# A hybrid attention layer: the second weight group is summed and split within the first projection step, two tiles of x are scaled next, and the rotation tables are loaded later

## The chip, the cores and the metric

The kernel runs on one core of a Trainium2 chip. TensorE (PE) multiplies matrices, VectorE (DVE), ScalarE (ACT) and GpSimd (POOL) do the elementwise work, SyncE (SP) issues transfers; sixteen DMA engines move the data. The metric is the device time of one execution in microseconds (us), the median of several.

## The reference

One layer over 1024 positions of width 1024, in float32:

```python
h = _rmsnorm(x, norm_gain[l])
proj = h @ w_in[l]
q_a, k_a, v_a, g_a, q_b, k_b, v_b, g_b = jnp.split(proj, split_at, axis=-1)
q_a = _rmsnorm(q_a.reshape(b, s, A_HEADS, HEAD_DIM), q_norm_a[l])
k_a = _rmsnorm(k_a.reshape(b, s, A_KV_HEADS, HEAD_DIM), k_norm_a[l])
q_a = q_a * cos + _rotate_half_axial(q_a) * sin
k_a = k_a * cos + _rotate_half_axial(k_a) * sin
o_a = _gqa_blocked(q_a, k_a, v_a) * jax.nn.silu(g_a)
o_b = _neighbourhood_attn(q_b, k_b, v_b, na_rpb[l]) * jax.nn.silu(g_b)
x = x + jnp.concatenate([o_a, o_b], axis=-1) @ w_out[l]
return _rmsnorm(x, final_norm_gain)
```

Group A is full attention with 8 query heads and 2 key heads, with normalised and rotated queries and keys. Group B is attention over a neighbourhood of a 16 x 64 grid. All that the change touches lies before the first scores of group A.

## The kernel before, in words

To keep float32 accuracy with float16 matmuls, every operand is split in two float16 parts: a high part (a scaled copy, rounded) and a low part (what the rounding left). A product is three matmuls: high by high, high by low, low by high.

The 1024 rows of x are eight tiles, numbered 0 to 7, of 128 rows. A tile passes through `load_x` (a transfer of 512 KB, SP's queue), `x_sq` (sum of squares, L289), `x_rs` (L296 on VectorE, then a power and a factor on POOL, L297 and L298), `x_y` (scaling on VectorE, L301; the high part on ScalarE, L302) and `x_lo` (the low part, L306). Each part is transposed by a transfer on SP's queue (`x_t`, L310) into `hT0` (high) or `hT1` (low). Four buffers hold tiles of x, so tile 4's load waits until tile 0 is done with.

The projection's 3328 columns are 13 groups of 256 (`raw0`, `raw1`, ... as loaded, `whl` as split). Preparing a group takes `prep_a` (squares, summed along a row: L344, L347, L364), `prep_b` (a matmul that adds the sums over the partitions, L373; then L375 on VectorE and a power on POOL, L376), `prep_c` (high parts on ScalarE, L382), `prep_d` (low parts on VectorE, L389) and `prep_e` (a few small factors, L421 to L428). From group 3 on the squares are L357 and the halves are split in quarters (L399, L404). Two buffers hold loaded groups and two hold split ones; group 2's split takes the place of group 0's. `load_w` (L207, POOL's queue, 1 MB) fetches groups from 2 on; for groups 2 and 3 a small copy on POOL (L206) ahead of it waits until tiles 6 and 5 of x have been measured.

Group 0 holds the keys and values of A (`kva_gen`), groups 1 and 2 its queries (`qa_gen`). TensorE takes pairs of row tiles: a pair is 48 matmuls of 128 x 256 for one group, and `proj_pair` yields after each six. TensorE's order is written out: pair 0 of group 0, pair 0 of group 1, pair 1 of each, then pairs 2 and 3 of group 0, pairs 2 and 3 of group 1, then group 2. `Flow.step(8)` issues eight such chunks with what is due beside them; `Flow.fill(n)` issues n chunks alone. After a pair `norm_rope` reads the result (L536, L537), normalises it (L540, L541 on VectorE, the power L542 on POOL, L546) and rotates it (L550 and L554 on POOL, L553 on VectorE) with the tables `tabs`. The tables come by `tables_in` (L259, L261, SP's queue) and are multiplied by the gains in `tables` (L265 to L275, VectorE) and `scale_tab` (L278, POOL, four times). Keys, queries and their low parts are transposed by SP's queue too (L573, L606, L608).

Within the block `tc.manual_schedule(engines={act, dve, pool, sp})` the four engines take their instructions in the order of the code. Outside it a scheduler orders them, and TensorE's order alone is that of the code. Every engine works through its own order strictly: an instruction that waits holds up all behind it.

Of the kernel before, what the change touches and what calls it, by code (L numbers as in the profile page):

```python
# [137 lines left out]
def kernel(ctx: ExitStack, tc: tile.TileContext, x: bass.AP, w: bass.AP, wo: bass.AP,  # L138
# [3 lines left out]
    act, dve, pool, pe, sp = nc.scalar, nc.vector, nc.gpsimd, nc.tensor, nc.sync  # L142
# [10 lines left out]
    fl = Flow()  # L153
# [66 lines left out]
    def load_x(u):  # L220
        xts.append(w4(u % NX, [P, 1024], F32, f"x{u}"))
        (act if u == 0 else sp).dma_start(xts[u], rows_of(x, u, 1024, 0, 1024))
# [35 lines left out]
    def tables_in():  # L258
        sp.dma_start(qkg, dap(qk_gain, 0, [[0, P], [D, 4], [1, D]]))  # L259
        for k in range(2):  # L260
            sp.dma_start(tabs[:, k], rope[k])  # L261
# [22 lines left out]
    def x_sq(u, e):  # L284
        xhl[u] = carve(ar, MIX + 4096 * (u % 4), [2, 1024], F16)
        xr[u] = tn(f"xs{u}", 2, "xs")
        junk = xhl[u][:, 0].bitcast(BF16)
        if e is act:
            act.activation(junk, xts[u], AF.Square, accum_out=xr[u][:, :1])  # L289
        else:  # L290
            dve.tensor_tensor_reduce(out=junk, in0=xts[u], in1=xts[u], scale=1.0, scalar=0.0, op0=OP.mult,
                                     op1=OP.add, accum_out=xr[u][:, :1])

    def x_rs(u):
        t = xr[u]
        dve.tensor_scalar(t[:, :1], t[:, :1], 1.0 / 1024, EPS, op0=OP.mult, op1=OP.add)  # L296
        pool.tensor_tensor(t[:, 1:], t[:, :1], mh[:, :1], op=OP.pow)  # L297
        pool.tensor_tensor(t[:, 1:], t[:, 1:], col(GX), op=OP.mult)  # L298

    def x_y(u):  # L300
        dve.scalar_tensor_tensor(xts[u], xts[u], xr[u][:, 1:], gain, op0=OP.mult, op1=OP.mult)  # L301
        act.activation(xhl[u][:, 0], xts[u], AF.Copy)  # L302
        x_t(u, 0)

    def x_lo(u, e):
        e.tensor_tensor(xhl[u][:, 1], xts[u], xhl[u][:, 0], op=OP.subtract)  # L306
        x_t(u, 1)
# [112 lines left out]
    def prep_e(g):  # L420
        dve.reciprocal(col(RC + g), col(S_ + g))  # L421
        if g < 13:
            dve.tensor_scalar(col(RC + g), col(RC + g), col(GXI), None, op0=OP.mult)
        if g in (KVA, QA, QA + 1):
            t = col(EC + g)
            dve.reciprocal(t, col(RC + g))
            dve.tensor_tensor(t, t, t, op=OP.mult)
            dve.tensor_scalar(t, t, EPS, None, op0=OP.mult)  # L428
        if g >= GATE and g < 13:
            dve.tensor_scalar(col(G2 + g - GATE), col(RC + g), 0.5, None, op0=OP.mult)  # L430
        if g == KB + 1:
            fin_scales()
        if GB <= g < 13:
            vfac(g - GB)
# [126 lines left out]
    def qa_gen(hh, up):  # L561
        def evac(pt):
            g = QA + hh
            stg = slot("stg1", [P, 2, 4, P], F16)
            a, b = (0, D) if hh == 0 else (D, 0)

            def fin(q):
                d = 4 if hh else 2
                at(d, "pre", lambda: act.activation(stg[:, :, :, a:a + D], q, AF.Copy))
                at(d, "mid", lambda: dve.tensor_tensor(stg[:, :, :, b:b + D], q, stg[:, :, :, a:a + D], op=OP.subtract))  # L570

                def tr():
                    sp.dma_start_transpose(qTa[hh][:, 2 * up:2 * up + 2].rearrange("p i h t -> p (i h) t"),  # L573
                                           stg.rearrange("p i a b -> p (i a b)"))
                at(d, "post", tr)
            norm_rope(g, up, pt, 4, 0, fin)
        yield from proj_pair(QA + hh, up, from_h, evac)
# [128 lines left out]
    def group(g, gens):  # L706

        def first(gen):
            prep(g + 1)
            yield from gen  # L710
        return [first(gens[0]) if g < 16 else gens[0], *gens[1:]]
# [297 lines left out]

    UP = range(4)  # L1010
    PAIR = 8.0
    with tc.manual_schedule(engines={act.engine, dve.engine, pool.engine, sp.engine}):
        x_sq(0, act)
        scale_gain()
        prep_a(0)
        load_w1(2, 3)
        x_rs(0)
        x_y(0)
        prep_a2(0)
        prep_b(0)  # L1020
        x_sq(1, act)
        prep_c(0)
        x_rs(1)
        load_x(2)
        x_lo(0, dve)
        x_y(1)
        load_x(3)
        prep_a(1)
        x_lo(1, pool)
        prep_d(0)  # L1030
        tables_in()
        x_sq(2, act)
        load_x(4)
        x_rs(2)
        load_x(5)
        prep_e(0)
        x_sq(3, act)
        x_y(2)
        x_rs(3)
    k, q = [kva_gen(up) for up in UP], group(1, [qa_gen(0, up) for up in UP])  # L1040
    fl.add(k[0], q[0], k[1], q[1], k[2], k[3], q[2], q[3], *group(2, [qa_gen(1, up) for up in UP]))
    fl.step(PAIR)
    prep_b(1)
    prep_c(1)
    x_y(3)
    x_lo(3, dve)
    x_sq(4, act)
    tables()
    scale_tab(2)
    x_rs(4)  # L1050
    x_y(4)
    x_lo(4, dve)
    x_lo(2, dve)
    x_sq(5, act)
    x_rs(5)
    load_x(6)
    scale_tab(0)
    x_y(5)
    prep_d(1)
    x_sq(6, act)  # L1060
    x_lo(5, dve)
    x_rs(6)
# [230 lines left out]
```

## Time and profile before

| what | value |
|---|---|
| time, three runs | 569.99 us median (568.47 to 571.41) |
| the profiled execution | 570.9 us, of which the span of instructions 569.1 us |
| PE busy | 516.9 us (91%), 5583 matmuls |
| DVE busy | 444.3 us (78%) |
| ACT busy | 368.7 us (65%) |
| POOL busy | 154.2 us (27%) |
| mean granted clock of PE | 0.973 |
| until 86.6 us | projections of A's keys and queries |
| 86.6 to 365 us | A's attention, the other projections in between |
| 365 to 569 us | B's attention, the output projection, the final norm |

An instruction row gives its start and length, engine, line, operation, output and inputs by the program's names (buffer numbers left out) and a count of those merged; in brackets stands how long the engine was idle before it and what ended that. Every operation in a helper has the helper's line, so L489 is every projection's matmul and L310 every transposed part of x.

### The profile page before, as it was taken

What the parts mean: (1) busy time and instruction counts of PE and PEld (TensorE: products, weight loads), DVE (VectorE), ACT (ScalarE), POOL (GpSimd) and SP (SyncE); (2) the same over time, 40 slices, a digit from 0 to 9 for tenths busy, and PEclk for the clock granted to TensorE, in tenths of its full rate; (3) what the DMA queues carried; (4) which work ended last, traced back from release to release, by engine and by line L of the source; (5) the groups of instructions that cost most, each with busy time, mean ns of one, the idle gap of its engine ahead of it and who ended that gap; (6) DMA issues with size and microseconds to landing.
All of it is one profiled execution on the core that took longest, in us unless ns stands there. A gap on an engine that the chain in (4) does not pass through costs nothing.

```text
span 569.1 us, 13780 instructions
## 1 busy us (share of the span) xinstructions
PE 516.9 (91%) x5583; PEld 403.1 (71%) x5583; DVE 444.3 (78%) x911; ACT 368.7 (65%) x583; POOL 154.2 (27%) x181
## 2 busy tenths in 40 slices
PE   2567989989999999999999999997999888999994
PEld 0455877768887555578888888886777566778883
DVE  3689688989977978788789897578788886987632
ACT  5546466958869669686786868285876686663211
POOL 2394887670000000000000034433621221213100
PEclk9978899999999999999999999999899798999998
DMA  8999739789999999998999989336576999998712
GB/s 242 214 182 225 128 61 212 126 144 182 228 229 185 172 213 196 197 186 162 237 162 200 187 185 184 97 75 155 125 128 114 192 199 204 164 149 156 202 38 74
DMA packets 244513, 95.47 MB, mean 168 GB/s; under 512 B 235489, under 2 KB 236001, under 8 KB 242530
## 3 DMA queue, kind: packets, MB, share of 16 engines
q1 hardware_dynamic: 240850, 73.89, 71.2%
q0 software_dynamic: 3312, 19.92, 12.6%
q10 hardware_dynamic: 288, 0.79, 0.5%
q8 instruction: 43, 0.70, 0.5%
q14 instruction: 20, 0.16, 0.1%
HBM read 29.56 MB, written 4.19 MB: 59 GB/s over the span
## 4 chain that ended last, share of the span: by engine, by line
PE 51%; DVE 11%; ACT 5%; issue 5%; DMA 5%; POOL 1%; SPq 0%; DVEq 0%; POOLq 0%; ACTq 0%
PE pj L489 19%; PE kb L489 7%; PE pjb L489 5%; DMA ar<-ar 4%; PE s L720 4%; PE s L722 4%; PE sb L489 3%; DVE ar L831 3%; PE pv L753 3%; PE pv L754 3%; PE pv L752 3%; ACT rq L833 2%; DVE ar L840 2%; DVE whl L404 1%; ACT ar L835 1%
## 5 line engine op out<-in xcount | busy, mean ns | idle before, releaser
L489 PEld LDWEIGHTS <-hT 128*128 128x128 f16 x2112 | 206.1, 100 | 61.3 <-DMA hT<-ar 17.3
L489 PE MATMUL pj<-whl,hT 128*128 128x256 f16 x1680 | 201.2, 278 | 22.4 <-DMA hT<-ar 10.4
L729 ACT ACTIVATE ar<-s,nm,sm 128x1024 f32<-128x1024 f32 x64 | 76.9, 1202 | 55.0 <-DVE nm L727 54.5
L727 DVE CUSTOM_DVE_ANT_0 ar<-s,sm 128x1024 bf16<-128x1024 f32 x64 | 82.0, 1281 | 32.4 <-PE s L722 32.1
L489 PEld LDWEIGHTS <-ar 128*128 128x128 f16 x768 | 74.6, 99 | 11.2 <-issue 2.2
L735 DVE TENSOR_TENSOR ar<-ar 128x1024 f16<-128x1024 f32 x64 | 79.5, 1242 | 1.4 <-ACT ar L730 1.4
L730 ACT ACTIVATE ar<-ar 128x1024 f16<-128x1024 f32 x64 | 67.6, 1057 | 2.1 <-DVE sum L759 0.3
L833 ACT ACTIVATE rq<-ar,nm 128x384 f32<-128x384 f32 (+1 forms) x64 | 34.1, 579 | 33.4 <-DVE nm L831 32.8
L489 PE MATMUL pjb<-whl,ar 128*128 128x256 f16 x408 | 48.9, 278 | 0.0
L489 PE MATMUL kb<-hT,whl 128*128 128x512 f16 x192 | 44.5, 379 | 0.0
L840 DVE SCALAR_TENSOR_TENSOR ar<-rq,ar 128x768 f16<-128x768 f32 (+1 forms) x32 | 30.8, 962 | 15.8 <-ACT ar L835 15.5
L753 PE MATMUL pv<-va,ar 128*128 128x64 f16 x384 | 40.0, 194 | 0.0
L752 PE MATMUL pv<-va,ar 128*128 128x65 f16 x384 | 39.9, 193 | 0.0
L754 PE MATMUL pv<-va,ar 128*128 128x65 f16 x384 | 39.8, 192 | 0.0
L752 PEld LDWEIGHTS <-ar 128*128 128x128 f16 x384 | 35.5, 96 | 5.3
L404 DVE SCALAR_TENSOR_TENSOR whl<-raw,sm,whl 128x512 f16<-128x512 f32 x52 | 39.1, 790 | 0.0
L753 PEld LDWEIGHTS <-ar 128*128 128x128 f16 x384 | 35.3, 97 | 5.3
L720 PE MATMUL s<-kTa,rq 128*128 128x512 f16 x128 | 38.0, 379 | 0.0
L207 POOL DMA_DIRECT2D raw<-in_w_dram x11 | 6.7, 608 | 111.3 <-ACT ar L730 89.0
L489 PE MATMUL pjb<-whl,hT 128*128 128x256 f16 x288 | 35.5, 281 | 0.0
L754 PEld LDWEIGHTS <-ar 128*128 128x128 f16 x384 | 35.4, 99 | 0.0
L874 POOL TENSOR_TENSOR ar<-ar,qkg 128x256 f32<-128x256 f32 x16 | 17.5, 1091 | 65.6 <-DVE qkg L872 64.4
(173 smaller groups left out, 972.7 us busy)
## 6 DMA issues: line engine op xcount, KB each, us to landing
raw<-in_w_dram POOLq DMA_DIRECT2D x11, 1024.0 KB, 7.4
raw<-in_wo_dram POOLq DMA_DIRECT2D x4, 1024.0 KB, 5.4
ar<-in_x_dram SPq DMA_DIRECT2D x7, 512.0 KB, 6.6
khh<-ar SPq DMA_DIRECT2D x16, 128.0 KB, 3.3
x2b<-in_x_dram POOLq DMA_DIRECT2D x4, 512.0 KB, 5.8
x<-in_x_dram POOLq DMA_DIRECT2D x4, 512.0 KB, 6.8
out_dram<-x2b SPq DMA_DIRECT2D x8, 256.0 KB, 3.6
out_dram<-x SPq DMA_DIRECT2D x7, 256.0 KB, 2.9
```

Source lines behind the costliest of these rows:

```text
L404: dve.scalar_tensor_tensor(wp[g][1][:, q], raw[g][:, q], col(S_ + g), wp[g][0][:, q], op0=OP.mult, op1=OP.subtract)
L489: pe.matmul(*o[0], **o[1])
L720: pe.matmul(s[:, c * 512:(c + 1) * 512], q, kTa[:, 4 * c:4 * c + 4, hh], start=True, stop=False)
L727: dve.tensor_tensor_reduce(out=hl[:, 1].bitcast(BF16), in0=s, in1=col(SHA).to_broadcast([P, 1024]), scale=col(NSA), scalar=3e38, op0=OP.ad ...
L729: act.activation(p32, s, AF.Exp, bias=nm, scale=col(SCA))
L730: at(0, "mid", lambda: act.activation(hl[:, 0], p32, AF.Copy))
L735: dve.tensor_tensor(hl[:, 1], p32, hl[:, 0], op=OP.subtract)
L752: pe.matmul(o, pt[:, kt], va[:, kt, hh, v_hi], start=kt == 0, stop=False)
L753: pe.matmul(o[:, :D], pt[:, kt], va[:, kt, hh, v_lo], start=False, stop=False)
L754: pe.matmul(o, pt[:, 8 + kt], va[:, kt, hh, v_hi], start=False, stop=kt == 7)
L833: act.activation(p32[:, e], t[:, e], AF.Exp, bias=nm, scale=-1.0)
L840: dve.scalar_tensor_tensor(hl[:, 1], p32, 2.0 ** 14, hl[:, 0], op0=OP.mult, op1=OP.subtract)
```

## The change

The generators of the first projections are made before the block that is ordered by hand, and one chunk of six matmuls is issued inside that block (`fl.fill(1)`), with `prep_b(1)` right behind it; the step that follows issues seven chunks instead of eight. `prep_c(1)` and `prep_d(1)` come into the block, ahead of the third and behind the fourth tile's load. The low part of tile 1 moves from POOL to VectorE. `x_lo(2)`, `x_y(3)` and `x_lo(3)` come into the block, right behind group 1's split. `tables_in` moves from ahead of tile 2's squares to behind tile 3's, past two loads of x. What is left outside the block is in the same order as before.

```diff
--- before.py
+++ after.py
@@ -1009,6 +1009,8 @@
 
     UP = range(4)
     PAIR = 8.0
+    k, q = [kva_gen(up) for up in UP], group(1, [qa_gen(0, up) for up in UP])
+    fl.add(k[0], q[0], k[1], q[1], k[2], k[3], q[2], q[3], *group(2, [qa_gen(1, up) for up in UP]))
     with tc.manual_schedule(engines={act.engine, dve.engine, pool.engine, sp.engine}):
         x_sq(0, act)
         scale_gain()
@@ -1026,37 +1028,36 @@
         x_y(1)
         load_x(3)
         prep_a(1)
-        x_lo(1, pool)
         prep_d(0)
-        tables_in()
+        x_lo(1, dve)
         x_sq(2, act)
         load_x(4)
+        fl.fill(1)
+        prep_b(1)
         x_rs(2)
+        prep_c(1)
+        x_y(2)
         load_x(5)
+        prep_d(1)
+        x_sq(3, act)
+        tables_in()
+        x_rs(3)
+        x_lo(2, dve)
+        x_y(3)
         prep_e(0)
-        x_sq(3, act)
-        x_y(2)
-        x_rs(3)
-    k, q = [kva_gen(up) for up in UP], group(1, [qa_gen(0, up) for up in UP])
-    fl.add(k[0], q[0], k[1], q[1], k[2], k[3], q[2], q[3], *group(2, [qa_gen(1, up) for up in UP]))
-    fl.step(PAIR)
-    prep_b(1)
-    prep_c(1)
-    x_y(3)
-    x_lo(3, dve)
+        x_lo(3, dve)
+    fl.step(PAIR - 1)
     x_sq(4, act)
     tables()
     scale_tab(2)
     x_rs(4)
     x_y(4)
     x_lo(4, dve)
-    x_lo(2, dve)
     x_sq(5, act)
     x_rs(5)
     load_x(6)
     scale_tab(0)
     x_y(5)
-    prep_d(1)
     x_sq(6, act)
     x_lo(5, dve)
     x_rs(6)
```

How the instructions then stand. First VectorE from the scaling of tile 1 (`xs1`) on; `xs2` to `xs7` are the other tiles' factors, `whl1` and `raw1` group 1, `pv0` where its sum arrives. Before:

```order
L301 SCALAR_TENSOR_TENSOR ar_78<-ar_78,xs1_134,gain_p_81 128x1024
L389 SCALAR_TENSOR_TENSOR whl0_118<-raw0_90,sm_97,whl0_118 128x2048
...
L301 SCALAR_TENSOR_TENSOR ar_78<-ar_78,xs2_157,gain_p_81 128x1024
...
L301 SCALAR_TENSOR_TENSOR ar_78<-ar_78,xs3_169,gain_p_81 128x1024
...
L306 TENSOR_TENSOR ar_78<-ar_78 128x1024
L375 TENSOR_SCALAR wss1_149<-pv0_101 128x1
...
L389 SCALAR_TENSOR_TENSOR whl1_148<-raw1_94,sm_97,whl1_148 128x1024
```

Now:

```order
L301 SCALAR_TENSOR_TENSOR ar_78<-ar_78,xs1_134,gain_p_81 128x1024
L389 SCALAR_TENSOR_TENSOR whl0_118<-raw0_90,sm_97,whl0_118 128x2048
L306 TENSOR_TENSOR ar_78<-ar_78 128x1024
L375 TENSOR_SCALAR wss1_149<-pv0_101 128x1
...
L301 SCALAR_TENSOR_TENSOR ar_78<-ar_78,xs2_154,gain_p_81 128x1024
L428 TENSOR_SCALAR sm_97<-sm_97 128x1
L389 SCALAR_TENSOR_TENSOR whl1_148<-raw1_94,sm_97,whl1_148 128x1024 x2
L296 TENSOR_SCALAR xs3_178<-xs3_178 128x1
L306 TENSOR_TENSOR ar_78<-ar_78 128x1024
```

Group 1's sum is read ahead of tile 2's scaling instead of behind tile 3's, and its low parts follow tile 2's scaling.

Second POOL, from the first products of the tables (`tabs`) on. `nt0_0` and `nt0_1` are the norms of pairs 0 and 1 of group 0, `nt1_0` and `nt1_1` those of group 1; `raw2` and `raw3` are the next two weight groups. Before:

```order
L278 TENSOR_TENSOR tabs_98<-tabs_98,qkg_85 128x512
...
L554 TENSOR_TENSOR ar_78<-ar_78 128x256
L298 TENSOR_TENSOR xs6_278<-xs6_278,sm_97 128x1
L206 COPY raw2_306<-xs6_278 128x1
L206 COPY raw3_311<-xs5_266 128x1
L207 DMA raw2_306<-in_w_dram 128x2048
L207 DMA raw3_311<-in_w_dram 128x2048
L297 TENSOR_TENSOR xs7_292<-xs7_292,mh_83 128x1
L298 TENSOR_TENSOR xs7_292<-xs7_292,sm_97 128x1
L542 TENSOR_TENSOR nt1_0_380<-nt1_0_380,mh_83 128x8
L550 TENSOR_TENSOR ar_78<-ar_78,tabs_98 128x8x32 x2
```

Now:

```order
L542 TENSOR_TENSOR nt0_1_446<-nt0_1_446,mh_83 128x4
L550 TENSOR_TENSOR ar_78<-ar_78,tabs_98 128x8x32 x2
L554 TENSOR_TENSOR ar_78<-ar_78 128x256
L206 COPY raw2_306<-xs6_278 128x1
L206 COPY raw3_311<-xs5_268 128x1
L298 TENSOR_TENSOR xs7_292<-xs7_292,sm_97 128x1
L550 TENSOR_TENSOR ar_78<-ar_78,tabs_98 128x4x32 x2
L542 TENSOR_TENSOR nt1_1_512<-nt1_1_512,mh_83 128x8
L554 TENSOR_TENSOR ar_78<-ar_78 128x512
L207 DMA raw2_306<-in_w_dram 128x2048
L207 DMA raw3_311<-in_w_dram 128x2048
```

The two weight loads (L207) stand behind the powers of `nt1_0`, `nt0_1` and `nt1_1` and behind the rotation's products of pair 0 of group 1 and pair 1 of group 0; the powers of all three stood behind the loads before.

Third VectorE around the last tile of x, whose factor is `xs7`. Now:

```order
L301 SCALAR_TENSOR_TENSOR ar_78<-ar_78,xs7_292,gain_p_81 128x1024
L600 TENSOR_TENSOR ar_78<-ar_78 128x2x128
L600 TENSOR_TENSOR ar_78<-ar_78 128x256
L588 SCALAR_TENSOR_TENSOR va_104<-pj0_2_529,va_104 128x2x64 x2
L540 TENSOR_REDUCE nt0_2_578<-ar_78 128x4
L546 TENSOR_TENSOR ar_78<-ar_78,nt1_1_512 128x512
L306 TENSOR_TENSOR ar_78<-ar_78 128x1024
```

The low part of tile 7 (L306) stands behind the reading of group 0's pair 2 (L588) and behind L546, which takes `nt1_1` from POOL. Before, pair 2's reading came behind all low parts.

## The prediction, on record before the changed kernel ran

> **What bounds the kernel now.** I read the waits of TensorE over the first 90 us first, because the change touches only what is issued there, then the order in time of each engine, then the transfers. A wait row is: engine, tile and line, what it waited for, us in total, times, longest.
>
> ```profile
> PE pj L489 <- DMA hT<-ar: 10.4, 5, 3.7
> PE pj L489 <- ACT whl L382: 7.8, 2, 6.9
> ```
>
> TensorE in order of time (start, us, instruction, count, and in brackets the idle time before it and what ended it):
>
> ```profile
> 19.35 4.37 PE L489 MATMUL pj<-whl,hT 128*128 128x256 f16 x24 [3.09 <-DMA hT<-ar]
> 24.07 1.92 PE L489 MATMUL pj<-whl,hT 128*128 128x256 f16 x16 [0.36 <-DMA hT<-ar]
> ...
> 32.85 17.66 PE L489 MATMUL pj<-whl,hT 128*128 128x256 f16 x144 [6.85 <-ACT whl L382]
> 54.20 0.61 PE L489 MATMUL pj<-whl,hT 128*128 128x256 f16 x2 [3.69 <-DMA hT<-ar]
> ...
> 70.49 0.24 PE L373 MATMUL pv<-wss,mh 128*128 128x1 bf16 x4
> 70.59 5.40 PE L489 MATMUL pj<-whl,hT 128*128 128x256 f16 x48
> 75.83 0.17 PE L373 MATMUL pv<-wss,mh 128*128 128x1 bf16 x1
> ```
>
> A pair of row tiles is 48 matmuls. I call the pairs k0 to k3 (keys and values, group 0) and q0 to q3 (queries, group 1); the order is k0 q0 k1 q1 k2 k3 q2 q3. TensorE stands still 6.85 us between k0 and q0, for the split of weight group 1, and 3.69 us before k2, for the transposed fifth tile. Then it runs. The stretches below give busy time, instructions, granted clock, DMA share and GB/s:
>
> ```profile
> 53.60:60.40 6.80, 5.82 (x28) 0.52 1.15 180
> 126.70:365.00 238.30, 238.28 (x2841) 1.00 0.98 189
> ```
>
> After the second stall the clock was granted at 0.52; a matmul then takes 5.82/28 = 0.21 us, against 5.40/48 = 0.11 at full clock. From 126.7 us on TensorE never stops for 238 us. So what these pairs gain or lose by the time TensorE leaves them is what the kernel gains or loses, if the order behind them is the same; it is, from q2 on.
>
> **Part 1: the split of group 1 moves ahead.** ScalarE and VectorE in time:
>
> ```profile
> 18.47 0.19 ACT L344 ACTIVATION_READ_ACCUMULATOR whl<-raw 128x1 f32 x1
> ...
> 31.66 2.17 ACT L382 ACTIVATE whl<-raw,sm 128x1024 f16<-128x1024 f32 x2
> ```
> ```profile
> 26.30 1.28 DVE L301 SCALAR_TENSOR_TENSOR ar<-ar,xs,gain_p 128x1024 f32<-128x1024 f32 x1
> ...
> 27.75 1.22 DVE L306 TENSOR_TENSOR ar<-ar 128x1024 f16<-128x1024 f32 x1
> 28.88 0.15 DVE L375 TENSOR_SCALAR wss<-pv 128x1 f32<-128x1 f32 x1
> ```
>
> The sum of squares is there at 18.66, but the matmul that adds it over the partitions stood behind all of k0 and its reading (L375) came at 28.88, the high parts (L382) at 31.66. Now the matmul stands behind six matmuls of k0. It makes TensorE wait for 18.66; that costs nothing, since the low part of tile 0 was waited for until 19.35 anyway. With about 1.3 us for matmul, L375 and POOL's power, L382 runs from 20.0 to 22.2, and the low parts, behind x's third tile on VectorE, end near 24.7. q0 needs both from 25.7 (tile 1's low part, now VectorE's, comes by the 0.36 us earlier). **Price: q0 starts 7.1 us sooner**, in a clock that has no cause to drop.
>
> **Part 2: what k1 and q1 then wait for.** q0 ends at 25.7 + 5.4 = 31.1. k1 needs tiles 2 and 3 in both parts. The transfers do not come sooner, because the DMA engines are full:
>
> ```profile
> 14.37:25.84 11.47, 8.02 (x49) 5.71 (x50) 6.24 (x13) 6.30 (x9) 4.51 (x5) 1.00 0.99 204
> 25.84:32.85 7.01, 0.16 (x4) 0.09 (x2) 6.94 (x23) 4.23 (x8) 3.74 (x3) 0.76 1.12 219
> ```
> ```profile
> 23.04 1.20 SPq L222 DMA_DIRECT2D ar<-in_x_dram  x2
> ```
> ```profile
> ar<-in_x_dram SPq DMA_DIRECT2D x2, 512.0 KB, 8.1
> ```
> ```profile
> 30.61 1.06 ACT L289 ACTIVATE ar<-ar 128x1024 bf16<-128x1024 f32 x1 [1.87 <-DMA ar<-in_x_dram]
> ```
>
> Share 0.99 and 1.12, some 0.21 MB per us. Tiles 4 and 5, issued at 23.04, landed 30.6 to 32. Now tile 4, the high part of tile 2 and tile 5 are ahead of the tables, 1.3 MB from 24: tile 5 lands at 30.4. Behind it come the tables (0.64 MB), tile 2's low part, tile 6, and tile 3's and 4's parts, together 2.2 MB by the low part of tile 3: 30.4 + 10.5 = 40.9. So k1's second half starts at about 41, and q1 ends at T = 40.9 + 2.7 + 5.4 = **49.0 against 50.5**. Of 7.1 us gained, 1.5 are left. k2 then follows without the 3.69 us and at full clock, to 54.4.
>
> **Part 3: the weight loads of groups 2 and 3 are issued later.** This decides. Before:
>
> ```profile
> 42.93 1.37 POOL L207 DMA_DIRECT2D raw<-in_w_dram  x2 [0.34 <-POOL raw L206]
> ```
> ```profile
> 43.18 1.25 SPq L310 DMA_TRANSPOSE hT<-ar  x1
> ```
> ```profile
> hT<-ar SPq DMA_TRANSPOSE x1, 11.0
> ```
> ```profile
> q0 software_dynamic: 124, 1.02, 85.3%
> q1 hardware_dynamic: 96, 0.02, 3.1%
> ```
> ```profile
> hT<-ar SPq DMA_TRANSPOSE x1, 2.7
> ```
>
> The last four come from the issues at 43.0 to 44.4, the queues in 44.5 to 48, and the issue at 59.12. Beside the two loads of 1 MB a transpose issued at 43.18 landed after 11.0 us; without them one takes 2.7. The loads moved 1.02 MB while the transposes moved 0.02. TensorE got tile 4's low part at 55.19, that is 12.2 us after the loads' issue R. The Trainium skill (DMA: Bandwidth & Descriptors, section Queues, rings and completion order) says that an engine takes turns between its queues packet by packet; 124 packets against 96 are such turns. By a reading in which turns are worth equal bytes the sum would be that of the sharing rival below.
>
> In the new order of POOL both loads stand behind all four table products (L278), three powers of the rotations (L542) and the whole rotation of q0. The rows for these:
>
> ```profile
> 29.67 4.69 POOL L278 TENSOR_TENSOR tabs<-tabs,qkg 128x512 f32<-128x512 f32 x3
> ...
> 37.61 1.26 POOL L278 TENSOR_TENSOR tabs<-tabs,qkg 128x512 f32<-128x512 f32 x1
> ...
> 39.67 0.86 POOL L550 TENSOR_TENSOR ar<-ar,tabs 128x128 f32<-128x128 f32 x2
> ...
> 41.34 0.73 POOL L554 TENSOR_TENSOR ar<-ar 128x256 f32<-128x256 f32 x1
> ...
> 51.55 2.56 POOL L542 TENSOR_TENSOR nt<-nt,mh 128x8 f32<-128x8 f32 x1 [4.08 <-DVE nt L541]
> 55.20 1.85 POOL L550 TENSOR_TENSOR ar<-ar,tabs 128x256 f32<-128x256 f32 x2 [1.09 <-DVE nt L541]
> 57.02 1.00 POOL L542 TENSOR_TENSOR nt<-nt,mh 128x4 f32<-128x4 f32 x1
> 57.99 1.25 POOL L554 TENSOR_TENSOR ar<-ar 128x512 f32<-128x512 f32 x1
> 59.22 1.82 POOL L542 TENSOR_TENSOR nt<-nt,mh 128x8 f32<-128x8 f32 x1
> ```
>
> Start: tile 5 landed 30.4, ScalarE's square 1.3, then on VectorE two low parts (1.22 each), one scaling (1.28) and some fifteen small ones (about 1.0): the tables' gains are ready at 36.4. POOL's sum: L278 4.69 + 1.26; L542 2.56 + 1.00 + 1.82; L550 0.86 + 1.85 + 0.86; L554 0.73 + 1.25; four powers and factors of x and two copies, 1.8: **18.7, so R = 55.1 against 42.93**. Bounds: tile 5 at 29 and every L542 at 1.00 make R = 51.3; two more us of waits or slow POOL work make 57.5.
>
> Which transposes now meet the loads? Those of tile 7. Its high part waits on ScalarE behind the reading of k2 (54.4 + 0.9) and takes 1.1: SyncE has it at 56.5, R + 1.4. Its low part stands on VectorE behind an instruction that waits for the last L542, the same that frees the loads 1.3 us later, so it cannot be issued before them; I take R + 2.9. Before, tile 4's parts stood alike to R (0.25 and about 3.5), so I take the same 12.2: **tile 7 is whole at R + 12.2 = 67.3**, while k3's first half is over near 58.7 (tile 6 is scaled just after q1 is read and is whole near 56). TensorE stands 8.6 us. The 24 matmuls of the second half cost 2.6 at full clock and 5.0 at 0.52; after the first stall the low clock lasted from 32.85 into this row, some 3.8 us, and 18 matmuls at the one price and 6 at the other make 4.5:
>
> ```profile
> 36.00:37.00 1.00, 1.00 (x9) 0.87 0.75 259
> ```
>
>  The Trainium skill (TensorE: Matmul & The Clock Gate, section What's actually happening) gives about 3.4 us of work until the clock is full: that would make about 4.3; the row at 53.60 to 60.40 shows longer.
>
> k3 ends at R + 16.7 = 71.8. Before:
>
> ```profile
> 53.93 0.63 ACT L357 ACTIVATE va<-raw 128x512 bf16<-128x512 f32 x1 [1.51 <-DMA raw<-in_w_dram]
> ...
> 57.02 0.63 ACT L357 ACTIVATE va<-raw 128x512 bf16<-128x512 f32 x1
> ...
> 68.07 1.91 ACT L344 ACTIVATE whl<-raw 128x2048 bf16<-128x2048 f32 x1 [3.70 <-PE pj L489]
> ```
>
> L344 shares its buffer with group 0 and starts when k3 is done: 68.0. **Sum: 71.8 - 68.0 = 3.8 us slower.** Behind that the same chain follows in both: L344, the sums in q2 and q3, L382, group 2's queries. The squares of group 3 (L357), landing 11.0 us after R and 3.8 long, end near 70 to 73 with the work between them, before the sum in the middle of q2 (74.4) asks for them.
>
> **Costed at nothing.** The tables come some four microseconds later on SP; their first user on POOL starts at 36.4 for other reasons. If that cover went, R would grow by as much. Tile 4's scale no longer waits behind the tables on POOL; tile 4 is transposed long before k2 instead of just in time, and this is the 3.69 us already counted.
>
> **Rivals.** (a) *R is small*: POOL's work runs at its short rows, R = 51.3 to 54, tile 7 is still held up: by R + 16.7 - 68.0 it is 0 to 2.8 slower, 570 to 572.8. For it: two L542 rows at 1.00 and 1.82; against: all of them stretched where VectorE was busy. (b) *The queues share*: tile 7 lands some 5 us sooner and k3 is done near 66; then the sum in the middle of q2 waits for L357, at R + 11.0 + 3.8 = 69.9 against 70.49: 0.6 faster, 569.4. Against: 0.02 MB beside 1.02. (c) *The filled gap is kept*: the queues share, and R comes under 52.8; from that point the same formula gives more than 2.8 us; at R = 51.3 it is 66.1 against 70.49, 4.4 faster, 565.6. It needs both, in one run. (d) *The sum of group 1 doesn't come sooner*, for a wait in k0 that I don't see: nothing gained, loads late all the same, 570 to 574.
>
> **How the numbers follow.** The sum is made in the profiled execution: 570.9 + 3.8 = 574.7; that execution lies 0.9 above the median of the runs, so the median comes to 570.0 + 3.8 = **573.8**. Chances: forecast 0.60, (a) 0.18, (b) 0.10, (c) 0.10, (d) 0.02. The likeliest one's own range is 572.8 to 576.4. The range takes in (a), (b) and R up to 57.5 with a microsecond for the clock, and leaves out (c): 568.5 to 577.5. About 0.5%, 2.85 us, is what can be told from no change: slower 0.60, same 0.30, faster 0.10.
>
> **What would show it.** q0 starting at 26 and the wait on L382 there gone; k1 waiting for hT at about 31 and 39; the first L207 at 53 to 57; a wait of TensorE on hT of 6 us or more that ends near 67; L344 at 70 to 73. Wrong would be: L207 before 51, or transposes issued beside the loads that land within 5 us.

## The result, and the profile after

The changed kernel takes 578.62 us (576.08 to 581.7, four executions) beside 570.27 us for the kernel before; the ratio is 1.0125, interval 1.0076 to 1.0175: **slower**, by more than was forecast. By the ratio the forecast's 570.0 us become 577.1, just within the range; the median of the four lies 1.1 us above it. The profiled execution, the second shortest of the four, took 576.29 us, span 574.5: 5.4 more than the 569.1 before. A ratio leaves out every execution more than 1.5% above the fastest of the same kernel (the profiled one of the kernel before with loads by ScalarE among them, so its span is not compared), and the table of the experiments says on how many it rests. Medians are over all executions, and every row is from a kernel's one profiled execution.

TensorE of the changed kernel in order of time, the rows that answer to those from 19.35 to 54.20 before:

```profile
24.68 7.38 PE L489 MATMUL pj<-whl,hT 128*128 128x256 f16 x66 [1.07 <-DMA hT<-ar]
33.06 2.58 PE L489 MATMUL pj<-whl,hT 128*128 128x256 f16 x22 [1.01 <-DMA hT<-ar]
37.74 0.39 PE L489 MATMUL pj<-whl,hT 128*128 128x256 f16 x2 [2.10 <-DMA hT<-ar]
39.48 14.94 PE L489 MATMUL pj<-whl,hT 128*128 128x256 f16 x120 [1.36 <-DMA hT<-ar]
55.18 2.58 PE L489 MATMUL pj<-whl,hT 128*128 128x256 f16 x22 [0.76 <-DMA hT<-ar]
62.26 0.61 PE L489 MATMUL pj<-whl,hT 128*128 128x256 f16 x2 [4.50 <-DMA hT<-ar]
67.23 6.66 PE L489 MATMUL pj<-whl,hT 128*128 128x256 f16 x46 [4.37 <-DMA hT<-ar]
```

The 6.85 us in front of q0 are gone. A tile takes 24 matmuls; from k1 on the first two need its high part alone, and 22 stand behind its low part. The 120 matmuls from 39.48 are 22 of k1's second half, q1, k2 and the first two of k3; the two rows behind tile 6's 22 are k3 waiting for tile 7, 4.50 us for its high part and 4.37 for its low part. In the waits of the whole execution, 7.8 us on L382 have become 0.4, and 10.4 us on hT have become 18.1:

```profile
PE pj L489 <- DMA hT<-ar: 18.1, 8, 4.5
PE pj L489 <- ACT whl L382: 0.4, 1, 0.4
```

The loads of groups 2 and 3, two rows of the transfer view (KB each, median us from issue to landing; of what was issued from 56.2 to 57.2 and from 58.8 to 58.9), and the squares of group 2:

```profile
56.28 1.37 POOL L207 DMA_DIRECT2D raw<-in_w_dram  x2
```
```profile
raw<-in_w_dram POOLq DMA_DIRECT2D x2, 1024.0 KB, 7.6
```
```profile
hT<-ar SPq DMA_TRANSPOSE x1, 8.3
```
```profile
71.31 1.91 ACT L344 ACTIVATE whl<-raw 128x2048 bf16<-128x2048 f32 x1 [0.95 <-PE pj L489]
```

Tile 7's high part was issued at 56.14, 0.14 us ahead of the loads, and TensorE had it at 62.26. The low part, issued at 58.86, took 8.3 us beside the loads; 58.86 + 8.3 = 67.2 is when k3 goes on. L344 starts 3.2 us later than before. Those 3.2 us are still there at 127 us, where TensorE next stands, for the sum of group 5's squares (L375). First before, then after:

```profile
96.62 0.63 ACT L357 ACTIVATE va<-raw 128x512 bf16<-128x512 f32 x1 [2.21 <-DMA raw<-in_w_dram]
126.72 0.82 PE L489 MATMUL pj<-whl,hT 128*128 128x256 f16 x6 [2.73 <-DVE wss L375]
```
```profile
99.82 0.63 ACT L357 ACTIVATE va<-raw 128x512 bf16<-128x512 f32 x1 [2.65 <-DMA raw<-in_w_dram]
129.92 0.82 PE L489 MATMUL pj<-whl,hT 128*128 128x256 f16 x6 [2.73 <-DVE wss L375]
```

In both TensorE leaves that wait 30.10 us after ScalarE got the load of group 5 and went on. That load is issued behind group 3's split (L207, 87.35 before, 90.08 after) and so hands the delay of the first stage on. Another 2.2 us come later, as a sum of gains and losses. Two waits behind 130 us that the kernel before has not at the same places:

```profile
153.33 0.20 PE L752 MATMUL pv<-va,ar 128*128 128x65 f16 x1 [1.21 <-DMA ar<-ar]
467.26 0.20 PE L860 MATMUL pvb<-ar 128*128 128x65 f16 x1 [2.20 <-DMA ar<-ar]
```

### The profile page after: what moved, and what is told of

It is laid out like the page before. It is cut to its first block, busy times and chain, and to the rows that moved or that the text cites. A ratio compares the mean times of both kernels' runs of the same rounds, so it can differ in the third digit from the quotient of the medians.

```text
span 574.5 us, 13788 instructions
## 1 busy us (share of the span) xinstructions
PE 513.9 (89%) x5583; PEld 400.9 (70%) x5583; DVE 444.3 (77%) x912; ACT 368.1 (64%) x583; POOL 151.9 (26%) x180
## 4 chain that ended last, share of the span: by engine, by line
PE 50%; DVE 10%; DMA 7%; ACT 6%; issue 5%; POOL 1%; SPq 0%; DVEq 0%; POOLq 0%; ACTq 0%
PE pj L489 17%; PE kb L489 7%; DMA ar<-ar 7%; PE pjb L489 5%; PE s L720 4%; PE s L722 4%; PE sb L489 3%; DVE ar L831 3%; PE pv L753 3%; PE pv L752 2%; PE pv L754 2%; ACT rq L833 2%; DVE ar L840 1%; ACT ar L835 1%; DVE mhl L913 1%
## 5 line engine op out<-in xcount | busy, mean ns | idle before, releaser
L489 PE MATMUL pj<-whl,hT 128*128 128x256 f16 x1680 | 200.8, 277 | 22.7 <-DMA hT<-ar 18.1
L727 DVE CUSTOM_DVE_ANT_0 ar<-s,sm 128x1024 bf16<-128x1024 f32 x64 | 81.9, 1280 | 32.4 <-PE s L722 30.2
L489 PEld LDWEIGHTS <-ar 128*128 128x128 f16 x768 | 73.8, 98 | 10.4 <-issue 2.1
L489 PE MATMUL pjb<-whl,ar 128*128 128x256 f16 x408 | 47.4, 273 | 0.0
L207 POOL DMA_DIRECT2D raw<-in_w_dram x11 | 6.7, 608 | 112.9 <-ACT ar L730 89.0
L874 POOL TENSOR_TENSOR ar<-ar,qkg 128x256 f32<-128x256 f32 x16 | 17.4, 1090 | 68.5 <-DVE qkg L872 59.1
```

Of the source, the lines that this page charges most:

```text
L489: pe.matmul(*o[0], **o[1])
L727: dve.tensor_tensor_reduce(out=hl[:, 1].bitcast(BF16), in0=s, in1=col(SHA).to_broadcast([P, 1024]), scale=col(NSA), scalar=3e38, op0=OP.ad ...
```

## The experiments

For each profiled execution three times say where it stands against the kernel before: the start of L344 (68.07 before), TensorE's leaving of the wait on L375 (126.72), and the span (569.1). The ratio is that of the timed executions. Where it leaves many out, the median beside it says what all of them took.

| kernel | L344 | wait on L375 left | span | median us | ratio, interval | executions in the ratio |
|---|---|---|---|---|---|---|
| the change | +3.2 | +3.2 | +5.4 | 578.62 | 1.0125, 1.0076 to 1.0175 | 4 of 4 |
| the change again | +3.6 | +3.1 | +5.6 | 578.39 | 1.0134, 1.0095 to 1.0173 | 4 of 4 |
| change, loads ahead of the tables | -0.5 | +1.0 | +3.8 | 574.08 | 1.0004, 0.9975 to 1.0034 | 7 of 12 |
| before, loads late | +2.9 | +1.9 | +3.8 | 573.89 | 1.0041, 1.0021 to 1.0061 | 9 of 9 |
| before, tables later alone | +5.3 | +5.3 | +5.3 | 577.59 | 1.0101, 1.0073 to 1.013 | 7 of 8 |
| before, early split alone | +2.8 | +2.5 | +4.3 | 573.68 | 1.0029, 1.0007 to 1.0052 | 10 of 10 |
| change, tables as before | +9.1 | +9.2 | +10.4 | 581.23 | 1.0131, 1.0077 to 1.0186 | 4 of 4 |
| change, one load later still | +6.5 | +4.5 | +6.1 | 582.78 | 1.0209, 1.0181 to 1.0236 | 4 of 4 |
| loads ahead and tile 7 early | +4.4 | +7.3 | +7.9 | 580.55 | 1.0034, 0.9987 to 1.0082 | 4 of 12 |
| change, loads by ScalarE | +4.8 | +5.6 | +4.1 | 576.13 | 1.01, 1.0059 to 1.0141 | 4 of 4 |
| before, loads by ScalarE | -1.4 | -0.4 | | 572.21 | 0.9986, 0.9959 to 1.0014 | 9 of 10 |
| tile 7 early, loads by ScalarE | -5.3 | -1.1 | +0.5 | 576.25 | 0.9986, 0.9953 to 1.0018 | 5 of 10 |
| the same, next loads by SP | -5.6 | -7.2 | -7.1 | 571.21 | 0.9898, 0.9852 to 0.9943 | 6 of 12 |

The kernel before, timed beside them, had medians of 570.27 to 572.55 us.

### Is it the late loads?

**The change once more, unedited.**

> The changed kernel once more, unedited. Its four executions lay in two groups, 576.1 to 576.3 and 581.0 to 581.7. Theory one (the second group is a delay in a later stage, which a transfer or the clock sets now and then): both groups come again, and a profile that falls in the upper one shows the 5 us in one or two stages behind 85 us. Theory two (chance of the chip in one session): all executions lie within 2 us of each other. The first stage should repeat: loads at 56, tile 7 whole at 67, L344 at 71.

It repeats: loads issued at 56.19, one wait of 8.07 us that ends at 66.75. (The high part of tile 7, issued 0.7 us ahead of the loads, came through this time.)

```profile
66.75 7.54 PE L489 MATMUL pj<-whl,hT 128*128 128x256 f16 x46 [8.07 <-DMA hT<-ar]
```

Its four executions (576.47 to 583.09) spread as the first four did, but not in two groups; the profiled one was the shortest, so neither theory on the spread is settled.

**The change with the loads right behind the first table product.** POOL's order is written out from `fl.step` on (a second block ordered by hand, for POOL alone), with the other three table products behind the loads; the loads wait for the gains of that first product. The main lines:

```diff
-            pool.tensor_copy(raw[g][:, 0, :1], xr[gate[g]][:, 1:])
+            pool.tensor_copy(raw[g][:, 0, :1], qkg[:, gate[g], :1])
...
+    with tc.manual_schedule(engines={pool.engine}):
+        fl.step(PAIR - 1)
...
+        scale_tab(2)
+        x_rs(6)
+        gate[2] = gate[3] = 2
+        load_w(2)
+        load_w(3)
...
```

> The changed kernel, but POOL has the two loads of groups 2 and 3 right behind the first table product: issued near 40 and 44 instead of 56.3. The early split of group 1 stays. Theory (the loss comes from the late loads, which hold up tile 7's transposes): the wait of TensorE for tile 7 that ended at 67.2 now ends by 62, L344 starts at 64 to 66 (71.3 in the changed kernel, 68.1 before), and the kernel takes 566 to 570 us, 3 to 6 under the kernel before the change plus 5, that is faster than before by up to 0.7%. Rival one (the collision only moves): tiles 5 and 6 meet the loads, TensorE waits in k2 or k3 until R + 12 = 52 to 56, L344 at 68 to 70, 572 to 575 us. Rival two (the loss lies in what comes later, not in the loads): L344 is sooner, but the time stays at 575 to 580.

Issued at 39.61 and 42.43, the loads were over by 51.7. Of the 8.9 us in front of k3's second half 3.5 are left, and the loss is gone from the seven executions of the ratio (1.0004; the median of all twelve is 574.08, beside 571.93 for the kernel before). L344 is only 0.5 us sooner than before, against the 64 to 66 expected: tile 7 was now late by its own preparation, its transposes issued at 58.42 and 59.78 (2.7 and 2.8 us without a load beside them), and k3 went on at 62.63 in a low clock (0.58 from 61 to 66 us). The time was not in the 566 to 570 expected either.

```profile
61.21 0.39 PE L489 MATMUL pj<-whl,hT 128*128 128x256 f16 x2 [2.48 <-DMA hT<-ar]
62.63 8.12 PE L489 MATMUL pj<-whl,hT 128*128 128x256 f16 x46 [1.03 <-DMA hT<-ar]
```

**The kernel before with the loads late.** Both wait for the power of q0's norm; the squares of group 3 are issued where they were. The main lines:

```diff
-            pool.tensor_copy(raw[g][:, 0, :1], xr[gate[g]][:, 1:])
+            pool.tensor_copy(raw[g][:, 0, :1], gate[g])
...
-    gate[2] = 6
...
-    load_w(2)
-    gate[3] = 5
     x_lo(7, dve)
-    load_w(3)
+    squares(3, 4)
 
     for p in range(8):
         fl.step(PAIR)
+        if p == 1:
+            gate[2] = nts[1, 0][:, 1, :1]
+            load_w(2)
+        if p == 1:
+            gate[3] = nts[1, 0][:, 1, :1]
+            load_w(3)
```

> The kernel before the change, with one thing changed: both loads are held until the first power of q0's norm is made on POOL, so they are issued at 54 to 55 instead of 42.9. Group 1 is split as late as before. Theory (late loads alone cost the time): the stall of 3.69 us ahead of k2 is gone, k2 starts at 50.6; a part of tile 7 stands behind the loads and is whole at R + 12 = 66 to 67; L344 starts at 70 to 71.5, the kernel takes 572 to 574 us (2 to 3.5 slower than before). Rival one (tile 7 gets through ahead of the loads): k3 ends near 62 and L344 waits for its load, R + 11 = 65 to 66: 567 to 569 us. Rival two (the loss of the change has nothing to do with the loads): 570 us as before.

Issued at 54.65, they put a wait of 3.89 us in front of tile 7's 22 matmuls and L344 at 71.00: late loads alone make the kernel slower, by 0.4%, as that theory had it. It loses less than L344 says, since group 5's load came without much of a wait (1.09 us instead of 2.21) and TensorE waited 0.76 us for L375.

```profile
66.22 7.37 PE L489 MATMUL pj<-whl,hT 128*128 128x256 f16 x46 [3.89 <-DMA hT<-ar]
```
```profile
98.49 0.63 ACT L357 ACTIVATE va<-raw 128x512 bf16<-128x512 f32 x1 [1.09 <-DMA raw<-in_w_dram]
128.61 0.81 PE L489 MATMUL pj<-whl,hT 128*128 128x256 f16 x6 [0.76 <-DVE wss L375]
```

**Two parts of the change alone in the kernel before**: the later tables, and the early sum and split.

```diff
-        tables_in()
         x_sq(2, act)
         load_x(4)
...
         x_sq(3, act)
         x_y(2)
+        tables_in()
```
```diff
...
         load_x(4)
+        fl.fill(1)
+        prep_b(1)
         x_rs(2)
+        prep_c(1)
         load_x(5)
+        prep_d(1)
         prep_e(0)
...
-    fl.step(PAIR)
-    prep_b(1)
-    prep_c(1)
+    fl.step(PAIR - 1)
...
-    prep_d(1)
```

> The kernel before, with one part of the change alone: the rotation tables are loaded later, behind x's fifth and sixth tiles; group 1 is split as late as before. Theory (R decides): the table products start near 36.5, the loads stand behind the power of k1's norm, R near 53, a part of tile 7 meets them and is whole near 65 to 66, L344 at 69 to 71, 571.5 to 574 us. Rival: 570 as before, if R is under 48.

> The kernel before, with the other part alone: the sum and the split of group 1 within k0; tables, x's tiles and their places stay as they were. Theory (R decides): q0 starts near 26, the loads are issued at 44 to 47, tile 6 meets them and is whole at 57 to 59, tile 7 at 60 to 62, L344 at 64 to 66, 566 to 570 us: this part alone makes the kernel up to 0.7% faster. Rival (the early split costs time behind 85 us by itself): L344 early, but 572 to 580 us with a spread of 5 us or more.

The tables' move alone puts the loads at 56.77 and costs 1.0%, more than expected and nearly the whole loss. The early split alone (its generators too are made ahead of the block) issues them at 49.41 and 50.92, and its 7 us are not kept either, against the expectation: TensorE waits 2.96 us for tile 5's low part, issued at 48.91, and some more for tiles 6 and 7, and L344 starts at 70.87.

```profile
56.77 1.37 POOL L207 DMA_DIRECT2D raw<-in_w_dram  x2
67.17 0.61 PE L489 MATMUL pj<-whl,hT 128*128 128x256 f16 x2 [7.43 <-DMA hT<-ar]
```
```profile
56.19 4.24 PE L489 MATMUL pj<-whl,hT 128*128 128x256 f16 x22 [2.96 <-DMA hT<-ar]
```

**The change with the tables loaded where they were.**

```diff
         x_lo(1, dve)
+        tables_in()
         x_sq(2, act)
...
         x_sq(3, act)
-        tables_in()
```

> The changed kernel, with one part of the change undone: the rotation tables are loaded where they were before, ahead of x's fifth tile. POOL then makes the four table products earlier, and the loads stand ahead of q0's rotation. Theory (R decides): R near 47, tile 6 meets the loads and is whole at 58 to 59, tile 7 at 61 to 62, L344 at 64 to 66 (71.3 with the change whole): 567 to 570 us. Rival (the tables are not what makes the loads late, or the late stages cost the time): R above 52 or 575 us and more.

The loads went out at 50.61, 5.7 us sooner than in the change. But tile 5's low part was issued at 50.66, right beside them, and TensorE stood 12.85 us for it, longer than it stood for tile 7 in the change. From 54 to 59 us the DMA engines moved next to nothing, while VectorE and POOL were busy almost throughout (columns: stretch, length, busy us and count of PE, PEld, which is the loading of TensorE's weights, DVE, ACT, POOL; granted clock, DMA share, GB/s):

```profile
65.96 13.01 PE L489 MATMUL pj<-whl,hT 128*128 128x256 f16 x94 [12.85 <-DMA hT<-ar]
```
```profile
55.00:56.00 1.00, 0.00 (x0) 0.00 (x0) 1.00 (x2) 0.00 (x0) 1.00 (x2) 1.00 0.05 17
60.00:61.00 1.00, 0.00 (x0) 0.00 (x0) 1.00 (x2) 0.00 (x0) 1.00 (x2) 0.50 1.16 432
```

R fell between the two theories, and the time on the rival's side, by this wait and not by the late stages. The date of the loads decides only together with what they meet: "whole at R + 12.2" is no law.

**One of the two loads later still**, so that tile 7 meets one, not two. The main lines:

```diff
-    gate[3] = 5
     x_lo(7, dve)
-    load_w(3)
+    squares(3, 4)
...
+        if p == 3:
+            gate[3] = nts[1, 1][:, 1, :1]
+            load_w(3)
```

> The changed kernel, with the load of group 3 held behind the power of q1's norm, about 6 us after that of group 2, so that only 1 MB and not 2 MB stands beside tile 7's transposes. Theory (transposes get through when the bytes of the loads are out of the queues): 1 MB takes about 5 us at 0.2 MB per us, tile 7 is whole at R + 6 to R + 8 = 62 to 64 instead of 67.2, L344 at 66 to 68, 573 to 575 us in the level in which the changed kernel takes 576. Rival (the loads' number or queue matters, not their bytes; the second load holds up the rest): tile 7 whole at 66 to 68 as in the changed kernel, L344 near 71, 576 to 579.

Halving the bytes in the way (group 3's load at 61.88) brought tile 7 only 1.0 us, whole at 66.2 and not at the 62 to 64 expected. That speaks against a sharing by bytes, rival (b) of the prediction in another form. It is not a clean test: the high part, issued at 56.17, came at 65.13, later than beside two loads, but the low part was issued 1.4 us later than in the change, at 60.31, and took 5.8 us instead of 8.3. The kernel became slower, since group 3's squares now ended last, at 74.7.

```profile
65.13 0.61 PE L489 MATMUL pj<-whl,hT 128*128 128x256 f16 x2 [7.31 <-DMA hT<-ar]
```

### What is it in a load that holds a transpose?

**Loads ahead of the tables and tile 7 early** (from the kernel with the loads ahead: `load_x(6)` and `load_x(7)` in front of tile 4's transposes, group 3's squares a step later).

> As e1_loads_ahead (loads of groups 2 and 3 behind the first table product, early split of group 1), and beside it x's last two tiles are loaded ahead of the transposes of tile 4, and the squares of group 3 come a step later, so that ScalarE scales tile 7 right behind the reading of q1 and SyncE has its transposes ahead of those of the keys. In e1 tile 7 was whole at 62.6 only because its own preparation was late (its scale on VectorE at 54.2). Theory (what sets the stage is when the last tile is whole): loads at 39 to 43, tile 7 whole at 57 to 59, TensorE waits at most 2 us for it, L344 at 60 to 62 against 67.5 in e1 and 68.1 before; 562 to 566 us. Rival (the loads then collide with tiles 5 and 6, whose low parts come at R + 12 = 52 to 55): L344 at 64 to 66, 567 to 570 us. Rival two (what the early split costs lies behind 85 us): L344 early, time 570 to 580 with a wide spread.

The theory failed, and neither rival had the size. The loads, issued at 39.66 and 42.37, met tile 5's transposes, as the first rival feared; beside each other the second load took 17.4 us and the two transposes 19.9 in the median, and L344 came 4.4 us later than in the kernel before. The ratio of 1.0034 rests on four of twelve executions; the median of all is 580.55.

```profile
raw<-in_w_dram POOLq DMA_DIRECT2D x1, 1024.0 KB, 17.4
hT<-ar SPq DMA_TRANSPOSE x2, 19.9
```
```profile
59.75 0.61 PE L489 MATMUL pj<-whl,hT 128*128 128x256 f16 x2 [8.15 <-DMA hT<-ar]
```

**Loads issued by ScalarE instead of POOL**: one word in three kernels (the change, the kernel before, and the one with tile 7 early).

```diff
-        pool.dma_start(raw[g], w[g] if g < 13 else wo[g - 13])
+        (act if g in (2, 3) else pool).dma_start(raw[g], w[g] if g < 13 else wo[g - 13])
```

> The changed kernel, with one word altered: the loads of groups 2 and 3 are issued by ScalarE's queue, not by POOL's; the gates stay. ScalarE reaches them behind its L595, near 51.6 to 53, so R is some 4 us sooner than in the changed kernel (56.28). What it tells apart: in the experiment with the tables at their old place a load's packets stood 6 us while VectorE and POOL were both busy, so the long collisions could belong to POOL's queue. Theory S (it belongs to POOL's queue): issued by ScalarE the two loads land in 5 to 7 us each and tile 7's transposes, issued near 56 and 59, land within 6 us; tile 7 is whole by 64, L344 starts near 67 to 68, the time is 569 to 572. Theory Q (the prediction's: two queues take turns and a transpose loses, whoever issues the load): the loads are over near R + 11 = 63, tile 7's low part, issued near 59, lands after 64, L344 at 68.5 to 70, the time 571 to 575. A transpose of tile 6 or 7 issued within 4 us of the loads that takes 9 us or more is for Q, one under 6.5 us is for S.

> The kernel before, with one word altered: the loads of groups 2 and 3 are issued by ScalarE's queue behind its L595, near 44.8 and 46, instead of POOL's at 42.93. Theory S (the long collision belongs to POOL's queue): the loads land in 5 to 7 us, tile 4's transposes, issued near 43.2 and 46.4, land by 51.5 instead of 54.2 and 55.2, TensorE's 3.69 us in front of k2 shrink to 1 or less, L344 starts near 66, the time is 567 to 569.5. Theory Q (turns, whoever issues): tile 4's low part lands 12 us after R, at 56.9, TensorE waits 5 to 6 us there, L344 at 69 to 70, the time is 571 to 573.

> The kernel of the experiment with tile 7 early (loads ahead of the table products, x's last two tiles loaded early), with one word altered: the loads of groups 2 and 3 are issued by ScalarE's queue instead of POOL's, near 39.5 and 40.5 as there (39.66, 42.37). There a load took 17.7 us and tile 5's transposes 20 us, and TensorE stood 8.15 us. Theory S (the long collision belongs to POOL's queue): loads land within 9 us, near 49 to 51, tile 5's transposes within 9 us, the wait of 8.15 us is under 2, L344 starts at 63 to 67, the time is 563 to 568. Theory Q (turns, whoever issues the load): loads and tile 5's transposes again take 15 to 20 us, TensorE waits 6 to 9 us for hT near 51 to 60, L344 at 71 to 73, the time 573 to 580.

The answers differ. In the change the first load landed in 5.9 us, but ScalarE waited until 64.71 for the second, issued at 51.87; tile 6's transposes, issued with them at 50.87 and 52.30, took 14.0 and 13.2, and TensorE stood 10.90 us: against S by the mark set, but later than Q had it too (L344 at 72.9). In the one with tile 7 early the loads' 17.7 and 17.4 us became 8.4 in the median and the wait of 8.15 less than one, L344 at 62.77: as S had it, though the time did not follow. In the kernel before, L344 came 1.4 us sooner, near S's 66, and the time is the same within its interval. There the loads also went out 1.3 us later (44.20), behind a transpose of 42.92 that took 2.7, so the date and the queue are not told apart.

```profile
raw<-in_w_dram ACTq DMA_DIRECT2D x1, 1024.0 KB, 5.9
hT<-ar SPq DMA_TRANSPOSE x1, 14.0
```
```profile
64.88 10.59 PE L489 MATMUL pj<-whl,hT 128*128 128x256 f16 x72 [10.90 <-DMA hT<-ar]
64.71 0.63 ACT L357 ACTIVATE va<-raw 128x512 bf16<-128x512 f32 x1 [6.64 <-DMA raw<-in_w_dram]
```
```profile
60.16 10.44 PE L489 MATMUL pj<-whl,hT 128*128 128x256 f16 x94 [0.93 <-DMA hT<-ar]
62.77 1.91 ACT L344 ACTIVATE whl<-raw 128x2048 bf16<-128x2048 f32 x1 [3.84 <-PE pj L489]
```

So the issuing queue matters in the kernel with tile 7 early, but loads issued by ScalarE collide as well. The Trainium skill (SBUF — State Buffer, section Summary: rules for kernel authors) says that VectorE, in some of its modes, holds up transfers issued by GpSimd, and never contends with those issued by ScalarE or SyncE; the row of 14.0 us shows that a transpose beside a load by ScalarE is held up all the same, so that this is not the whole cause. What the rest is stays open.

### Where does a gain of the first stage go?

The kernel with tile 7 early and loads by ScalarE was 5.3 us ahead at L344, and only 1.1 us at the wait on L375. Between lies group 5's load, issued 0.2 us behind a transpose of group 2's queries (L573), and both took 12.5 us:

```profile
raw<-in_w_dram POOLq DMA_DIRECT2D x1, 1024.0 KB, 12.5
rq<-ar SPq DMA_TRANSPOSE x1, 12.6
```
```profile
95.48 0.63 ACT L357 ACTIVATE va<-raw 128x512 bf16<-128x512 f32 x1 [5.60 <-DMA raw<-in_w_dram]
125.60 0.81 PE L489 MATMUL pj<-whl,hT 128*128 128x256 f16 x6 [2.75 <-DVE wss L375]
```

Again 30.12 us from the one to the other; over the thirteen profiles so far it was 30.10 to 30.12 (counted from the landing itself it is 30.2, not the 29.9 of the expectation below), so this arrival looks to be what sets where TensorE stands at 127 us. **The next two loads in the transposes' own queue:**

```diff
-        (act if g in (2, 3) else pool).dma_start(raw[g], w[g] if g < 13 else wo[g - 13])
+        (act if g in (2, 3) else sp if g in (4, 5) else pool).dma_start(raw[g], w[g] if g < 13 else wo[g - 13])
```

> The kernel of the experiment with tile 7 early and loads by ScalarE, with the two next loads (groups 4 and 5) issued by SP's queue, ahead of the two transposes L573 of group 2's queries. There TensorE was 5 us ahead of the kernel before at 75 us and 1.1 us ahead at 125.6; between, the load of group 5 was issued 0.2 us behind a transpose L573 and both took 12.5 us (before: 9.2 and 9.6), and TensorE left its next wait (on L375) 29.9 us after that load landed, in the kernel before, in the changed one and there. Theory L (the first stage's gain is lost to that load's collision): in one queue the load isn't in a transpose's way; it lands within 6 to 7 us of its issue near 83, by 90 instead of 95.4, the transpose behind it lands near 91 to 92 instead of 95.4, ScalarE's wait of 5.6 us in front of L357 is under 1, TensorE leaves the wait on L375 at 120.5 to 122.5 instead of 125.6, and the profiled span is 564 to 567 instead of 569.6; ratio to the kernel before 0.989 to 0.995. Rival G (the stretch from 85 to 125 us is paced by something else, POOL's rotations or VectorE's reading of the scores): the load lands sooner, but TensorE leaves the wait at 125 to 126 all the same; span 569 to 570.

Theory L held, and went further. In one queue the load landed in 5.3 us and the transpose behind it in 7.3, both sooner than side by side; ScalarE no longer waited, and TensorE's 2.75 us became 0.18. The load was also issued 1.1 us sooner (81.83) and ahead of the transpose instead of behind it, so the queue and the order of the two are not told apart.

```profile
raw<-in_w_dram SPq DMA_DIRECT2D x1, 1024.0 KB, 5.3
rq<-ar SPq DMA_TRANSPOSE x1, 7.3
```
```profile
119.54 0.81 PE L489 MATMUL pj<-whl,hT 128*128 128x256 f16 x6 [0.18 <-DVE wss L375]
```

The profiled span is 562.0, 7.1 below the kernel before, and the ratio 0.9898 (0.9852 to 0.9943): the one kernel here with a ratio clearly below that of the kernel before. With a reserve: the ratio rests on six executions of twelve, and the median of all twelve is 571.21, beside 570.89 for the kernel before. So the gain is shown for those six, not for the kernel as a whole.

## Why the prediction was right in sign and too small in size

- **Part 1, q0 7.1 us sooner.** Right in kind. The 66 matmuls from 24.68 to 32.06 are 16 of k0, q0 and two of k1, so q0 started near 24.68 + 16 x 0.11 = 26.5, not 25.7: 6.4 us sooner. The rest is tile 1's low part, which came at 24.68 and not 0.36 us ahead of the 24.07 of before.
- **Part 2, T = 49.0.** Right by luck: ScalarE began to read q1 at 49.00. The low part of tile 3 was there at 39.48, 1.4 us sooner than the 40.9 reckoned. Against that the clock was granted at 0.50 to 0.52 from 39.5 to 43 us, behind the waits of 2.10 and 1.36 us, and TensorE ran some 21 matmuls in 3.5 us; the sum had a full clock there. The waits at 33.06, 37.74 and 39.48 add up to 4.5 us with the DMA engines full (share 1.14 and 1.29), as reckoned.
- **Part 3, R = 55.1.** Right, and in the way that was reckoned: POOL's first table product started at 36.98 (36.4 reckoned) and from there to the loads it took 19.3 us (18.7). R is 56.28, within the bounds, of which the upper one should read 57.1. The tables' move was costed at nothing, and as a delay of that first product it cost 1.3 us, the distance to the kernel with the move undone (the second row):

```profile
36.98 2.49 POOL L278 TENSOR_TENSOR tabs<-tabs,qkg 128x512 f32<-128x512 f32 x2 [0.77 <-DVE qkg L275]
35.70 2.49 POOL L278 TENSOR_TENSOR tabs<-tabs,qkg 128x512 f32<-128x512 f32 x2 [2.83 <-DVE qkg L275]
```

Yet undone it puts R at 50.61. The other 4.4 us are POOL's order: with the move undone q0's rotation (L550 on 128 x 256) stands behind the loads again, at 51.99; in the change it stands ahead of them, at 48.70. The sum had taken that order in; it did not say that it comes from the tables' move. Moved alone in the kernel before, the tables delay the first product too, from 29.67 to 40.57, and put R at 56.77.

- **Whole at R + 12.2.** Measured R + 10.95: 67.23. Both sizes were off, by 1.2 in opposite directions, and 67.3 was right only so, by luck. As a rule the step is wrong: transposes of x issued within 3 us behind a weight load took from 8.2 to 19.4 us in these runs, and 2.7 without one.
- **24 matmuls at 4.5 us, k3 done at 71.8.** Two of the 24 ran at 62.26, on the high part; the other 22 took 71.31 - 67.23 = 4.1, which is the reckoned price. TensorE stood 4.50 + 4.37 = 8.9 us for tile 7 instead of 8.6. The low clock did not end 3.8 us into the row: it held from 60.0 to 70.2 with TensorE busy 3.57 us of it. The 3.8 was a misreading too: 0.87 over the microsecond from 36 is about a quarter of it at half clock, so that the low clock ended 3.4 us behind 32.85.

```profile
60.00:70.20 10.20, 3.57 (x17) 2.23 (x18) 5.04 (x8) 3.75 (x11) 5.63 (x7) 0.50 0.99 251
```

The Trainium skill (TensorE: Matmul & The Clock Gate, section What's actually happening) gives about 3.4 us of work until the clock is full; TensorE worked from 67.23 to 70.2, 3.0 us, until it was, and the row at 36 us, read so, gives 3.4: both agree, and the one at 53.60 to 60.40 stays longer.

- **"Behind that the same chain".** The step that was too short. The 3.2 us do pass on, by group 5's load, to 127 us. Behind it the profile lost 2.2 more, and the change's second profile 2.5, but not at the same places: there the wait of 2.74 us that ends at 129.80 is followed by a low clock, which in the first profile it is not. First the change, then the change again:

```profile
129.90:136.00 6.10, 6.08 (x74) 4.81 (x75) 6.03 (x10) 5.25 (x8) 0.56 (x1) 1.00 1.18 168
129.90:136.80 6.90, 6.90 (x61) 4.89 (x61) 6.83 (x12) 6.02 (x9) 0.46 (x1) 0.77 1.11 172
```

In the table that last part goes from -1.5 (change, loads by ScalarE) to +2.8 (change, loads ahead), so it looks like scatter between executions, which was not shown. Of some 7.1 us in the ratio (0.0125 x 570) the late loads explain 3.2; the next 2.2 are seen and not explained, and the last 1.7 lie in executions that were not profiled.
- **The rivals.** (a) fell: R was not small. Against (b), sharing, stand the 8.3 us and the run with one load later. (c), the filled gap kept, needed more than early loads: the loads ahead gave 1.0004, the early split alone 1.0029. Only the last experiment kept it, with two further loads moved that no rival named. (d) fell: the 6.85 us in front of q0 went.

## What to carry to other kernels

When an edit fills a gap, list the transfers that its new order delays and look at which transposes they now run beside; here a table load moved past two others was enough by itself to cost 1.0%, because two weight loads went out later and met other transposes. A gain in one stage is kept only if the next thing that ends a wait comes sooner too: find it by a constant distance between an arrival and the wait that ends behind it (30.1 us here, in thirteen profiles). A large load and a transpose that must overlap in time may be better in one queue, the load first, than in two; one experiment here shows it.

## What the runs showed of the hardware that was not expected

- Group 5's load of 1 MB and a transpose, issued 0.2 us apart in two queues, took 8.1 to 12.6 us each in thirteen profiles (9.2 and 9.6 in the kernel before, at 87 us), longer than one behind the other in one queue (5.3 and 7.3). The Trainium skill (DMA: Bandwidth & Descriptors, section Rules for kernel authors) holds that spreading transfers over issuing engines only saves issue time; here the load's time to landing fell by 7 us in the last experiment, with the queue and the order of the two changed.
- The DMA engines can stand nearly idle with both in flight: share 0.05 and 17 GB/s at 55 us, then 432 GB/s at 60, in the kernel with the tables as before. The cause was not isolated.
- Taking half of the load out of the way (one load of two) brought the tile in question only 1.0 us (66.2 for 67.2).
